# A hybrid Fourier / RWKV-7 layer on one core: a table and two token tiles get longer rows, and what else is placed moves by 128, 192 or 384 bytes

## The chip, the cores and the metric

The kernel runs on one core of a Trainium2 chip. The time is that of one execution on the device, in microseconds (us), the median of several runs: 3869.45 us for the kernel before (three runs, 3867.17 to 3881.99). A single profiled execution took 3867.45 us, and its span from the first instruction to the last is 3865.6 us.

## The reference, cut to what matters

All arithmetic is float32. One layer, 256 context tokens and 2048 latent tokens, model width 1024:

```python
hx = modulate(rmsnorm(x, norm1_g), sh1, sc1)
px = hx @ w_in                       # 1024 x 4480: recurrent columns, Fourier columns, gates
qx = rwkv_inputs(centred_shift(px[..., :RWKV_COLS], mu_prev, mu_next), lp)
hc = modulate(rmsnorm(ctx, norm1_g), csh1, csc1)
pc = hc @ w_in[:, :RWKV_COLS]        # the context needs the recurrent columns alone
yx = bidir_wkv(qx, states of the context)      # decay, kd, v, kk, a: a scan over time, both ways
fx = fourier_latent(px[..., FOURIER_START:GATE_START], rows)
f_ = sigmoid(gate_f) * (fx @ w_up_f)
r_ = sigmoid(gate_r) * (rwkv_output(yx, qx) @ w_up_r)
x = x + ga1 * ((f_ + r_) @ w_out)
hx2 = modulate(rmsnorm(x, norm2_g), sh2, sc2)
x = x + ga2 * ((silu(hx2 @ w_gate) * (hx2 @ w_up)) @ w_down)     # hidden width 2816
return rmsnorm(x, final_norm_g)
```

## The kernel before, in words

**Precision by three matmuls.** Every large product is made by `mm3` (L152 to L157). Weights and activations are each split into a high and a low part of the type float32r, and each slice k of 128 input channels takes three matmuls: high weights by high activations (L155), high weights by low activations (L156), low weights by high activations (L157). Each matmul loads its own 128 x 128 weights first. The *weights* are the stationary operand; the *moving* operand is a row of an activation tile, 512 tokens long (256 or 258 in the second token tile of the projection).

**Weights.** `load_w` (L141 to L150) brings 128 columns of a weight matrix from DRAM in pieces of four slices (`wraw`), and makes the high part on ScalarE (`whi`, L148) and the low part on VectorE (`wlo`, L149). Two buffers of each, `[128, 8, 128]`, serve the whole kernel; a slice is 512 bytes long in each partition.

**Stages, in order of time.**

- *Projection.* The 2304 tokens go in three parts of 768. In each part the normed tokens stand in two pairs of tiles: `hh`, `hl` of 512 columns (the first pair), and `hh`, `hl` of 258 columns (the second pair), eight slices k in each. They are allocated at L365. The second pair has 258 columns since the first two parts need two tokens of the next one for the shift; the matmuls take 258 columns of it for the recurrent columns (`pxps`) and 256 for the gates and Fourier columns (`fps`).
- *Scan.* The recurrence, in blocks of 128 tokens, both directions at once. Its matmuls are plain float32 with 32 to 128 columns. `pcT` (L195) is the table of the products of decays over chunks of 64 tokens: 36 chunks, two directions, four pairs of heads. The projection writes it and the scan's `state` step reads it.
- *Fourier.* Small DFT matmuls (`hps`, `p12`), then `fx @ w_up_f` (`pf`, moving tiles `fh`, `fl`) with the group norms.
- *Merge.* `c_merge` (`pr`, moving `oh`, `ol`) and `c_out` (`po`, moving `mh`, `ml`), for four blocks of 512 tokens.
- *Feed-forward.* Two blocks of 1024 tokens, each as two halves of 512. For 128 hidden columns at a time, the gate weights go over the first half and then over the second (`pgt`, 24 matmuls each), then the up weights the same way (`put`); the moving tiles are `xh`, `xl` of that half. After six or five such column groups `pd` multiplies the hidden tiles `uh`, `ul` of both halves with `w_down`.

**Where tiles stand.** Tiles are placed by pools, one after another in each partition's memory. Pools of the left side grow from the low addresses: first the constants (`pcT` and `carry` are the last of them), then the weight buffers, then the pools of single stages (Fourier, `fmp`, and `fa`, which holds `xh` and `xl` of the first half). Pools of the right side are placed against the upper end: `hp` with the normed tokens and, below it, `px` with everything else of the projection; when they are closed, `sp` of the scan, later `ep` of the merge and `ff`'s pool (second halves, `uh`, `ul`) take the same room. So a longer tile on the left moves all that follows on the left, and a longer tile in `hp` moves what lies below it in `hp` and `px`, but nothing in `sp` or `ep`.

An instruction scheduler sets the order of the projection, the Fourier stage, the merge and the feed-forward; the scan's order is written by hand.

Of the kernel before, what the change touches and what calls it, by code (L numbers as in the profile page):

```python
# [7 lines left out]
F32 = mybir.dt.float32  # L8
F32R = mybir.dt.float32r
# [7 lines left out]
TOT = SEQ + CTX  # L17
KT = 8
# [4 lines left out]
C = 64  # L23
# [17 lines left out]
def layer_kernel(ctx: ExitStack, tc, I, out_T, dbg=None):  # L41
# [3 lines left out]
    cst = ctx.enter_context(tc.tile_pool(name="cst", bufs=1))  # L45
# [38 lines left out]
    hp = hpx.enter_context(tc.tile_pool(name="hp", bufs=1, side="right"))  # L84
# [56 lines left out]
    def load_w(src, K):  # L141
        hi = wp.tile([128, KT, 128], F32R, tag="whi", name="whi", bufs=2)
        lo = wp.tile([128, KT, 128], F32R, tag="wlo", name="wlo", bufs=2)
        for k0 in range(0, K, 4):
            k1 = min(K, k0 + 4)
            raw = wp.tile([128, 4, 128], F32, tag="wraw", name="wraw", bufs=RW)[:, 0:k1 - k0, :]
            nc.sync.dma_start(raw, src[:, k0:k1, :])
            nc.scalar.activation(out=hi[:, k0:k1, :], in_=raw, func=AF.Copy)  # L148
            nc.vector.tensor_tensor(out=lo[:, k0:k1, :], in0=raw, in1=hi[:, k0:k1, :].bitcast(F32), op=ALU.subtract)  # L149
        return hi, lo  # L150
# [41 lines left out]
                fo2[64 * h2:64 * h2 + 64, :].rearrange("p (a c) -> p a c", c=128))  # L192


    pcT = cst.tile([128, TOT // C, 2, 4], F32, name="pcT")  # L195


    carry = cst.tile([128, 15, 1], F32, name="carry")
# [1 line left out]
    with ExitStack() as st:  # L200
# [148 lines left out]

        def gate_columns(ct, H, lats):  # L350
            w = load_w(I["w_in"][ct], KT)
            for (hh, hl), (l0, n) in zip(H, lats):
                if l0 is None:
                    continue
                ps = pmm.tile([128, 512], F32, tag="mm", name="fps")
                mm3(ps[:, 0:n], w, lambda k: hh[:, k, 0:n], lambda k: hl[:, k, 0:n], KT, n)
                gate_evict(fo_tile, ct, ps, l0, n)

        NP = 3
        for part in range(NP):  # L360
# [1 line left out]
            S = [px.tile([128, 768], F32R, tag=f"S{i}", name=f"S{part}_{i}", bufs=1) for i in range(4)]  # L362

            cols = [(512, 256), (258, 0)] if part == 0 else [(512, p0), (258 if part < 2 else 256, p0 + 512)]
            H = [[hp.tile([128, KT, 512 - 254 * i], F32R, tag=f"h{y}{i}", name=f"h{y}{part}_{i}")[:, :, 0:n] for y in "hl"]  # L365
                 for i, (n, _) in enumerate(cols)]
            for i, (n, b0) in enumerate(cols):
                hh, hl = H[i]
                for c0 in range(0, n - n % 256, 256):
# [7 lines left out]
            if part < 2:  # L377
                for c0 in range(p0 + 768, p0 + 1536, 256):
                    xs = load_x(c0)
                    rs = stats(xs, c0, False)  # L380
                    if c0 == p0 + 768:
                        hh, hl = [x[:, :, 256:258] for x in H[1]]
                        xe = xs[:, :, 0:2]
# [18 lines left out]
            for ci, ct in enumerate((12, 13, 0, 8, 4, 1, 9, 5, 2, 10, 6, 3, 11, 7, 14)):  # L402
# [11 lines left out]
                for i, (n, _) in enumerate(cols):  # L414
                    hh, hl = H[i]
                    ps = ppx.tile([128, 512], F32, tag="px", name="pxps", bufs=6 - NAUX)
# [45 lines left out]
                for g in ((15 + ci, 30 + ci // 3) if ci % 3 == 2 else (15 + ci,)):  # L462
                    gate_columns(g, H, lats)

# [296 lines left out]
    with ExitStack() as st:  # L761
# [5 lines left out]
        for g in range(4):  # L767
# [5 lines left out]
            for (j0, j1) in ((0, 3), (3, 7), (7, 11), (11, 15), (15, 16)):  # L773
                ps = pmm.tile([128, 512], F32, tag="mm", name="hps")
                col = 0
                for j in range(j0, j1):
                    n = 192 if j == 0 else 128
# [351 lines left out]
```

## Time and profile before

| what | before |
|---|---|
| median of three runs | 3869.45 us |
| the profiled execution, its span | 3867.45 us, 3865.6 us |
| TensorE (PE) busy | 3486.3 us, 90% |
| VectorE (DVE), ScalarE (ACT) busy | 2028.1 us (52%), 1358.3 us (35%) |
| mean granted TensorE clock | 0.932 of full speed |
| projection, 66 to 1092 us | PE busy 977.3 of 1026 us |
| scan and Fourier transforms, 1092 to 1862 us | PE busy 576.0 of 770 us |
| `pf` and group norms, 1862 to 2014 us | PE busy 122.4 of 152 us |
| merge, 2014 to 2350 us | PE busy 298.6 of 336 us |
| feed-forward, 2395 to 3842 us | PE busy 1444.0 of 1447 us |

Times of stages are from the profiled execution's start. The end of a matmul is modelled in the profile (it is pipelined, and the next one starts before it ends), so a matmul's own duration is longer than the time it takes from the stream. The time from one start to the next, here called the *step*, is read from the list of instructions in order of time.

### The profile page before, as it was taken

To read this page: it belongs to the slowest core of one execution; us is meant where nothing else is said; L and a number is where in the kernel's file an instruction comes from. 1 tells how busy PE (TensorE), PEld (TensorE's weight loads), DVE (VectorE), ACT (ScalarE), POOL (GpSimd) and SP (SyncE) were. 2 spreads that over 40 slices of the span, in tenths; PEclk is the share of its full clock that TensorE was granted. 3 is DMA by queue.
4 is the path that set the end of the run, shared out by engine and by line. 5 is a ranking of instruction groups with operands and counts; after the bars stand their busy time and mean duration, and the time that the engine had idled before them with its cause. 6 is when DMAs were issued, how large, how long until landed. Compare 5 with 4: busy or idle time off the path is not lost.

```text
span 3865.6 us, 55086 instructions
## 1 busy us (share of the span) xinstructions
PE 3486.3 (90%) x21140; PEld 2867.7 (74%) x21140; DVE 2028.1 (52%) x4005; ACT 1358.3 (35%) x2632; POOL 472.7 (12%) x865
## 2 busy tenths in 40 slices
PE   5999899999958888886789798999999999999997
PEld 5786788878847777775567676888888878888886
DVE  5577557746667777762568654223233542222325
ACT  3567456645523433332234332212111321111122
POOL 0133223213221222210110000000000000000000
PEclk9999999999977888777889899999999999999998
DMA  5454544535454455534686554111111241111112
GB/s 179 125 167 149 161 144 169 168 103 177 152 161 114 130 133 142 143 85 127 226 270 225 169 185 144 46 54 41 52 45 52 84 140 42 52 45 48 50 47 68
DMA packets 270231, 465.48 MB, mean 120 GB/s; under 512 B 84208, under 2 KB 103664, under 8 KB 269456
## 3 DMA queue, kind: packets, MB, share of 16 engines
q1 hardware_dynamic: 230336, 334.38, 27.3%
q0 software_dynamic: 39632, 127.59, 10.4%
q8 instruction: 166, 2.72, 0.3%
q14 instruction: 97, 0.79, 0.1%
HBM read 341.64 MB, written 120.21 MB: 119 GB/s over the span
## 4 chain that ended last, share of the span: by engine, by line
PE 39%; issue 7%; DMA 3%; DVE 2%; ACT 1%; POOL 0%; SPq 0%; DVEq 0%; POOLq 0%; ACTq 0%
PE pd L155 4%; PE pd L156 4%; PE pd L157 4%; PE pgt L156 4%; PE put L157 4%; PE pgt L157 4%; PE pgt L155 4%; PE put L156 4%; PE put L155 4%; DMA wraw<-w_up_f 1%; DMA gnb<-y_dr 1%; DVE wlo L149 0%; POOL x_dr L921 0%; DMA x__21736<-x_dr 0%; DVE oo L1021 0%
## 5 line engine op out<-in xcount | busy, mean ns | idle before, releaser
L148 ACT ACTIVATE whi<-wraw 128x512 fp32r<-128x512 f32 (+2 forms) x642 | 360.6, 598 | 1074.8 <-PE pd L156 353.6
L149 DVE TENSOR_TENSOR wlo<-wraw,whi 128x512 fp32r<-128x512 f32 (+2 forms) x642 | 397.7, 651 | 354.0 <-ACT whi L148 353.0
L155 PE MATMUL pgt<-xh,whi 128*128 128x512 f32 x704 | 277.7, 395 | 12.4 <-ACT xh L879 12.4
L155 PE MATMUL fps<-hh,whi 128*128 128x512 f32 (+1 forms) x800 | 284.8, 356 | 0.0
L157 PE MATMUL fps<-hh,wlo 128*128 128x512 f32 (+1 forms) x800 | 284.7, 356 | 0.0
L156 PE MATMUL fps<-hl,whi 128*128 128x512 f32 (+1 forms) x800 | 282.5, 353 | 0.0
L156 PE MATMUL pd<-ul,whi 128*128 128x512 f32 x704 | 278.0, 395 | 0.0
L157 PE MATMUL pd<-uh,wlo 128*128 128x512 f32 x704 | 277.9, 395 | 0.0
L155 PE MATMUL pd<-uh,whi 128*128 128x512 f32 x704 | 277.5, 395 | 0.0
L155 PE MATMUL put<-xh,whi 128*128 128x512 f32 x704 | 277.3, 394 | 0.0
L156 PE MATMUL put<-xl,whi 128*128 128x512 f32 x704 | 277.1, 394 | 0.0
L157 PE MATMUL put<-xh,wlo 128*128 128x512 f32 x704 | 277.1, 394 | 0.0
L156 PE MATMUL pgt<-xl,whi 128*128 128x512 f32 x704 | 276.7, 393 | 0.1
L157 PE MATMUL pgt<-xh,wlo 128*128 128x512 f32 x704 | 276.7, 393 | 0.0
L155 PE MATMUL pxps<-hh,whi 128*128 128x512 f32 (+2 forms) x720 | 250.2, 348 | 18.8 <-ACT hh L229 11.3
L156 PE MATMUL pxps<-hl,whi 128*128 128x512 f32 (+2 forms) x720 | 248.5, 346 | 7.0 <-DVE hl L230 7.0
L1007 DVE SCALAR_TENSOR_TENSOR x1f<-pd,ga2h,x1f 128x512 f32<-128x512 f32 x128 | 96.1, 751 | 293.5 <-PE pd L157 293.5
L157 PE MATMUL pxps<-hh,wlo 128*128 128x512 f32 (+2 forms) x720 | 246.4, 344 | 0.0
L997 DVE TENSOR_TENSOR tg<-tg,put 128x512 f32<-128x512 f32 x88 | 60.4, 688 | 269.0 <-PE put L157 268.9
L156 PEld LDWEIGHTS fps<-hl,whi 128*128 128x128 f32 x800 | 151.8, 190 | 25.5 <-issue 5.5
L157 PEld LDWEIGHTS fps<-hh,wlo 128*128 128x128 f32 x800 | 151.8, 190 | 24.4 <-issue 4.4
L155 PEld LDWEIGHTS fps<-hh,whi 128*128 128x128 f32 x800 | 152.1, 190 | 23.7 <-issue 4.3
(382 smaller groups left out, 7183.8 us busy)
## 6 DMA issues: line engine op xcount, KB each, us to landing
wraw<-w_in SPq DMA_DIRECT2D x210, 256.0 KB, 3.1
wraw<-w_gu SPq DMA_DIRECT2D x176, 256.0 KB, 2.8
BD<-bd_dr SPq DMA_DIRECT2D x36, 512.0 KB, 6.8
KR<-kr_dr SPq DMA_DIRECT2D x36, 512.0 KB, 7.1
wada<-w_ada SPq DMA_DIRECT2D x32, 512.0 KB, 4.8
wraw<-w_out SPq DMA_DIRECT2D x64, 256.0 KB, 3.2
wraw<-w_down SPq DMA_DIRECT2D x64, 256.0 KB, 2.7
xs<-xT POOLq DMA_DIRECT2D x15, 1024.0 KB, 6.0
```

The source lines that it names most:

```text
L148: nc.scalar.activation(out=hi[:, k0:k1, :], in_=raw, func=AF.Copy)
L149: nc.vector.tensor_tensor(out=lo[:, k0:k1, :], in0=raw, in1=hi[:, k0:k1, :].bitcast(F32), op=ALU.subtract)
L155: nc.tensor.matmul(ps, wh[:, k, :], xh(k), start=start and k == 0, stop=False)
L156: nc.tensor.matmul(ps, wh[:, k, :], xl(k), start=False, stop=False)
L157: nc.tensor.matmul(ps, wl[:, k, :], xh(k), start=False, stop=stop and k == K - 1)
L997: nc.vector.tensor_tensor(out=tg, in0=tg, in1=pu, op=ALU.mult)
L1007: nc.vector.scalar_tensor_tensor(out=x1[:, ct, :], in0=pd, scalar=ga2h[:, ct:ct + 1], in1=x1[:, ct, :], op0=ALU.mult, op1=ALU.add)
```

## The change

Two tiles get longer rows than they use. `pcT` is placed as if it had 40 chunks instead of 36: 1280 bytes in each partition instead of 1152. The second pair `hh`, `hl` of the projection gets 264 columns instead of 258: a slice is 1056 bytes long instead of 1032, a tile 8448 instead of 8256. No computed value differs, and no other line is changed. In the two built programs the order of instructions is the same, row for row, on each engine.

```diff
-    pcT = cst.tile([128, TOT // C, 2, 4], F32, name="pcT")
+    pcT = cst.tile([128, TOT // C, 2, 4], F32, name="pcT", padded_shape=[128, 40, 2, 4])
...
-            H = [[hp.tile([128, KT, 512 - 254 * i], F32R, tag=f"h{y}{i}", name=f"h{y}{part}_{i}")[:, :, 0:n] for y in "hl"]
+            H = [[hp.tile([128, KT, 512 - 248 * i], F32R, tag=f"h{y}{i}", name=f"h{y}{part}_{i}")[:, :, 0:n] for y in "hl"]
                  for i, (n, _) in enumerate(cols)]
```

What moves is the place of tiles. The built programs give each tile's byte address in a partition; here it is modulo 256. "Distance" is that of the moving row from the weights' row, modulo 256; k is the slice, 0 to 7.

| tiles | before | after | distance before | distance after |
|---|---|---|---|---|
| `whi`, `wlo` (all stages) | 96 | 224 | | |
| first pair `hh`, `hl` (projection) | 96 | 224 | 0 | 0 |
| second pair, `hh` | 96 + 8k | 224 + 32k | 8k | 32k |
| second pair, `hl` | 160 + 8k | 224 + 32k | 64 + 8k | 32k |
| `fh`, `fl` (`pf`) | 96 | 224 | 0 | 0 |
| `oh`, `ol`, `mh`, `ml` (merge) | 224 | 224 | 128 | 0 |
| `xh`, `xl` of the first half | 96 | 224 | 0 | 0 |
| `xh`, `xl` of the second half | 224 | 224 | 128 | 0 |
| `uh`, `ul` (`pd`) | 224 | 224 | 128 | 0 |
| the scan's tiles | 224 | 224 | | |

The step from one slice to the next is 2048 bytes in the 512-column tiles and 512 bytes in the weights, so their rows all lie where the tile does, modulo 256. Tiles of the projection's other work move by 384 bytes, those of the Fourier stage and the group norms by 128.

## The prediction

> **What bounds the kernel now.** I read the page first, for the share of each engine and the costliest groups; then the table of busy time by stretch; then single stretches in order of time, for the step from one matmul's start to the next; last the table of waits of TensorE.
>
> The page:
>
> ```profile
> span 3865.6 us, 55086 instructions
> PE 3486.3 (90%) x21140; PEld 2867.7 (74%) x21140; DVE 2028.1 (52%) x4005; ACT 1358.3 (35%) x2632; POOL 472.7 (12%) x865
> PEclk9999999999977888777889899999999999999998
> ```
>
> The stretches (projection; scan and Fourier transforms; `pf`; merge with `pr`; merge with `po` alone; feed-forward). After the length come busy us and instructions of each engine, the granted clock, the share of the DMA engines and GB/s:
>
> ```profile
> 66.00:1092.00 1026.00, 977.29 (x5043) 800.45 (x5043) 660.69 (x1117) 603.34 (x1091) 270.38 (x485) 0.98 0.46 150
> 1092.00:1862.00 770.00, 575.99 (x7858) 513.04 (x7858) 488.63 (x1480) 262.05 (x643) 150.17 (x274) 0.77 0.46 127
> 1862.00:2014.00 152.00, 122.42 (x492) 92.18 (x492) 97.42 (x176) 50.79 (x105) 23.18 (x40) 0.90 0.79 261
> 2014.00:2255.00 241.00, 206.38 (x857) 160.67 (x858) 173.91 (x285) 94.64 (x176) 15.47 (x26) 0.91 0.66 219
> 2255.00:2350.00 95.00, 92.19 (x387) 73.25 (x385) 46.23 (x68) 29.72 (x52) 8.65 (x16) 0.98 0.41 136
> 2395.00:3842.00 1447.00, 1443.99 (x6239) 1170.59 (x6237) 486.60 (x767) 285.77 (x523) 0.00 (x0) 1.00 0.18 56
> ```
>
> TensorE is the bound outside the scan. In the feed-forward, 37% of the span, it is busy 1444.0 of 1447 us at the full clock, with VectorE at 486.6 and ScalarE at 285.8 us, so a nanosecond taken from each matmul there is taken from the end, and no other engine is near enough to take over. In the projection it is busy 95% and in the last piece of the merge 97%. The scan and Fourier stretch (TensorE 75%, clock 0.77) is bound otherwise.
>
> A busy matmul is not a matmul at its best, though. Here is one column group of the feed-forward in order of time: the first `pgt` of the first half, the first of the second half, and the first `put`, 24 matmuls between each and the next:
>
> ```profile
> 2459.45 0.39 PE L155 MATMUL pgt<-xh,whi 128*128 128x512 f32 x1
> ...
> 2464.90 0.39 PE L155 MATMUL pgt<-xh,whi 128*128 128x512 f32 x1
> ...
> 2470.49 0.39 PE L155 MATMUL put<-xh,whi 128*128 128x512 f32 x1
> ```
>
> The same weights, the same number of columns, no wait: the first half takes 5.45 us, a step of 227.1 ns, the second 5.59 us, a step of 232.9 ns. The first half's tiles lie at 96 modulo 256 like the weights (distance 0), the second half's at 224 (distance 128). Groups of the feed-forward over its whole length say the same in the modelled durations: `pd`, whose tiles are all at distance 128, has 395 ns, and `put`, half of whose matmuls are at distance 0, 392.
>
> ```profile
> L156 PE MATMUL pd<-ul,whi 128*128 128x512 f32 x704 | 278.0, 395 | 0.0
> L157 PE MATMUL pd<-uh,wlo 128*128 128x512 f32 x704 | 277.9, 395 | 0.0
> L155 PE MATMUL pd<-uh,whi 128*128 128x512 f32 x704 | 277.5, 395 | 0.0
> L157 PE MATMUL put<-xh,wlo 128*128 128x512 f32 x688 | 269.9, 392 | 0.0
> ```
>
> **The change part by part.** No instruction, wait or transfer is added, taken away or put elsewhere in order, on any engine or queue. What can change is how long an instruction takes, by where its operands lie. The forecast rests on one reading: the step is 227 ns where the moving row and the weights are at the same offset modulo 256, and about 6 ns more at distance 128. Step by step:
>
> *`pd`.* 8 column tiles by two halves by 6 slices by 3 are 288 matmuls without a break, 287 steps in 66.97 us:
>
> ```profile
> 2503.63:2570.60 66.97, 66.97 (x288) 1.00 0.17 52
> ```
>
> That is 233.3 ns. Brought to 227.1, each of the 2112 `pd` matmuls (three lines, 704 each) gives 6.2 ns: 13.1 us, all on the path.
>
> *Second halves of `pgt` and `put`.* Half of six lines of 704, so 2112 matmuls, 5.8 ns each: 12.2 us, on the path. The first halves keep distance 0 and give nothing.
>
> *`po`.* A block is 192 matmuls, 191 steps, in 44.45 us from the first row to the last:
>
> ```profile
> 2176.76 0.39 PE L155 MATMUL po<-mh,whi 128*128 128x512 f32 x1
> ...
> 2221.21 0.40 PE L157 MATMUL po<-mh,wlo 128*128 128x512 f32 x1
> ```
>
> 232.7 ns; 5.6 ns by 768 matmuls are 4.3 us. TensorE hardly waits in this piece (97% busy), so it counts in full.
>
> *`pr`.* 384 matmuls at the same distance give 2.2 us at the most. But here TensorE waits for others between them:
>
> ```profile
> PE pr L155 <- ACT oh L160: 20.8, 4, 14.2
> PE pr L155 <- ACT whi L148: 6.5, 5, 2.6
> PE pr L157 <- DVE wlo L149: 2.7, 2, 2.3
> ```
>
> Where the next weights or the next `oh` are late, a matmul that ends earlier only waits longer. Between 0 and 2.2 us; I take 1.1, since the waits fall on few of the column tiles.
>
> *The second pair of the projection.* Its rows were at distances 8k and 64 + 8k, and come to 32k, equal for `hh` and `hl`. One group of 24 matmuls with 256 columns, and one with 258, from the first row to the one behind the last:
>
> ```profile
> 593.44 0.28 PE L155 MATMUL fps<-hh,whi 128*128 128x256 f32 x1
> ...
> 596.28 0.39 PE L155 MATMUL fps<-hh,whi 128*128 128x512 f32 x1
> ...
> 631.62 0.28 PE L155 MATMUL pxps<-hh,whi 128*128 128x258 f32 x1
> ...
> 634.52 0.39 PE L155 MATMUL fps<-hh,whi 128*128 128x512 f32 x1
> ```
>
> Steps of 118.3 and 120.8 ns, against 113.6 and 114.4 if the 227.1 ns scaled with the columns. There are 1320 and 720 of them. If every distance that is a multiple of 32 did as well as 0, this gives 4.7 ns by 1320 and 6.4 by 720: 10.8 us. If each still paid the 6.2 ns of distance 128, it would cost 1.5 ns by 1320 and give 0.2 by 720: a loss of 1.8 us. Only k = 0 reaches distance 0 for certain; the other seven slices remain apart, and the trace has no row at 32, 96 or 160. I take 2 us, nearer to the lower end, since the present distances, all different, cost about the same 5 to 6 ns as 128 does in the large tiles: the toll looks like one per matmul that is not at 0.
>
> *All else.* `pf` and the first pair stay at distance 0, the scan's tiles do not move, `pcT` is read and written as before; VectorE, ScalarE and the DMAs work on rows of the same lengths at starts that move by multiples of 64 bytes. In the feed-forward and the projection these engines have room (the stretches above), so a change of theirs by a per cent would be hidden; I take nothing.
>
> The sum: 13.1 + 12.2 + 4.3 + 1.1 + 2 = 32.7 us. The profiled execution took 3867.45 us, 2 us below the median of the runs shown; 3867.45 - 32.7 is 3834.8, and half-way to the median's scale that is 3836 us.
>
> The Trainium skill says otherwise about the cause: "TensorE: Matmul & The Clock Gate", Part 2, Step-by-step, has two independent read ports on TensorE, one for the moving operand and one for loading weights, so that loading the next weights takes no read bandwidth from the running matmul. By that rule a distance between the two can cost nothing, and only the moving row's own place is left to explain 227.1 against 232.9 ns; that is the first rival, and by it the sum would be 30 us the other way.
>
> **The rivals.**
>
> *The moving row's own place counts, not the distance.* Then rows that start at 224 modulo 256 are slow whatever the weights do, and the change brings every 512-column tile to 224: the first halves of `pgt` and `put` (2112 by 5.8 ns: 12.2 us), the first pair of the projection (2520 matmuls, 14.6 us), `pf` (384, at most 2.2, half of it hidden like `pr`), with nothing won in `pd`, `po` and the second halves. About 28 us slower: 3895. For it: in the matmuls compared here the weights always stand at 96, so own place and distance never part. Against it: the second pair's rows cover the starts from 96 to 152 (`hh`) and 160 to 216 (`hl`), nearly up to 224, and in the group of 256 columns the two are alike:
>
> ```profile
> L156 PE MATMUL fps<-hl,whi 128*128 128x256 f32 x8 | 2.2, 281 | 0.0
> L155 PE MATMUL fps<-hh,whi 128*128 128x256 f32 x8 | 2.2, 280 | 0.0
> ```
>
> A toll that came from starting shortly before a 256-byte line should grow towards 216. It does not; what those rows share is that they are not where the weights are.
>
> *Neither counts: no change.* The 6 ns could come from something that the fast tiles share by chance, the pool they stand in or the rows' distance in higher address bits. Then nothing moves and the time stays at 3868. For it: only one stage, the feed-forward, holds both kinds side by side. Against it: the first pair of the projection stands far up in the right-hand pool, at byte 180064, and `uh` at 180192, 128 bytes on; so pool and higher address bits are the same, and only the place modulo 256 differs. Here is one group of 24 on the first pair, from its first row to the one behind its last:
>
> ```profile
> 282.13 0.40 PE L155 MATMUL fps<-hh,whi 128*128 128x512 f32 x1
> ...
> 287.59 0.39 PE L155 MATMUL pxps<-hh,whi 128*128 128x512 f32 x1
> ```
>
> 5.46 us, a step of 227.5 ns, where `pd` on `uh` has 233.3; and VectorE and ScalarE are busier around it than in the feed-forward.
>
> *The lock is imperfect.* At distance 0 everywhere but in the small tiles, steps could settle between 227 and 233. Half of the sum is 16 us: 3852. This is the upper part of the first case rather than a case of its own.
>
> **How the numbers follow.** The forecast (distance counts) has 0.67, its own range being 3822 (the 10.8 us of the small tiles and all of `pr` come on top: 43 us) to 3853. No change has 0.18, own place 0.15. So 3836 is the prediction. The range from 3822 to 3872 takes in the first two cases and leaves out the third with the edges of the first. About half a per cent, 19 us, is what a measurement of this kernel can tell from no change. Faster by more than that: 0.67, less 0.02 for an imperfect lock that keeps over half of the toll, 0.65. Slower by more: 0.15, own place. Within: the rest, 0.20.
>
> **What would show it.** If the distance counts, the durations of `pd` in the groups fall from 395 to about 389, like `put` and `pgt`; the second 24 matmuls of a column group take 5.45 us instead of 5.59; a run of 288 `pd` matmuls takes 65.2 us instead of 66.97; the feed-forward's stretch is 25 us shorter, the merge's some 5, and the scan's the same to the microsecond. The forecast is wrong if the first halves come to 233 ns with everything else as before (own place), or if the steps are untouched (neither). The small tiles' part is wrong, alone, if their groups of 24 do not come out about 0.02 us shorter than 2.84 and 2.90 us. If the steps fall and the time does not, something else in the feed-forward would have to show as a wait of TensorE, where now there is 3 us in 1447.

## The result, and the profile after

| what | before | after |
|---|---|---|
| median | 3869.45 us | 3846.74 us |
| ratio, 95% interval | | 0.9935 (0.9906 to 0.9963) |
| a second set of runs: median | 3878.61 us | 3844.98 us |
| its ratio, 95% interval | | 0.9913 (0.9900 to 0.9927) |
| the profiled execution | 3867.45 us | 3840.49 us |

The changed kernel is faster, by 0.65% in the first set and 0.87% in the second, where the interval is narrower. From profile to profile it is 27.0 us. The ratios are taken over all executions of a set but the slow ones (one of the kernel before, 5028.75 us, in the first set, and one of the kernel with rows of 1280 bytes below, 5740.91 us), so they are not just the quotients of the medians.

The page of the changed kernel, the lines that answer to those of before:

```profile
span 3838.7 us, 55086 instructions
PE 3455.2 (90%) x21140; PEld 2869.3 (75%) x21140; DVE 2028.0 (53%) x4005; ACT 1357.8 (35%) x2632; POOL 477.3 (12%) x865
PEclk9999999999976878876899899999999999999998
```

VectorE, ScalarE and the instruction counts are what they were; TensorE is 31 us less busy. Its groups in the feed-forward (line, operation, shapes, count, busy us and mean ns of one, idle time before and its releaser):

```profile
L156 PE MATMUL pd<-ul,whi 128*128 128x512 f32 x704 | 274.0, 389 | 0.0
L157 PE MATMUL pd<-uh,wlo 128*128 128x512 f32 x704 | 273.9, 390 | 0.0
L155 PE MATMUL pd<-uh,whi 128*128 128x512 f32 x704 | 273.6, 390 | 0.0
L155 PE MATMUL put<-xh,whi 128*128 128x512 f32 x688 | 268.1, 390 | 0.9 <-ACT whi L148 0.9
L157 PE MATMUL put<-xh,wlo 128*128 128x512 f32 x688 | 268.0, 390 | 0.0
```

`pd` came from 395 to 389 or 390 ns, `put` from 392 to 390, and there is no difference left between them. The same column group as before, in order of time (start us, modelled duration us, what):

```profile
2458.60 0.39 PE L155 MATMUL pgt<-xh,whi 128*128 128x512 f32 x1
...
2464.04 0.39 PE L155 MATMUL pgt<-xh,whi 128*128 128x512 f32 x1
...
2469.48 0.39 PE L155 MATMUL put<-xh,whi 128*128 128x512 f32 x1
```

Both halves now take 5.44 us for 24 matmuls, a step of 226.7 ns; before it was 5.45 and 5.59. The second half's tiles did not move. They stand at 224 modulo 256 as before, and only the weights came to them.

The time of each stage, from first and last starts in the two lists of instructions (projection: first `pxps` to last `fps`; scan: from there to the last `xr`; `pf` and group norms: first `pf` to first `pr`; merge: first `pr` to last `po`; feed-forward: first `pgt` to last `pd`), with the second trace of the changed kernel beside it:

| stage, us | before | after | after, second trace |
|---|---|---|---|
| projection | 1020.7 | 1022.1 | 1019.6 |
| scan | 679.7 | 681.5 | 688.2 |
| `pf` and group norms | 151.9 | 151.8 | 148.8 |
| merge | 335.2 | 330.5 | 333.3 |
| feed-forward | 1486.8 | 1459.9 | 1460.6 |

The gain lies in the feed-forward, 26.2 to 26.9 us of it. The merge gives 4.7 and 1.9 us. The scan, in which neither an instruction nor an address of its own tiles differs, was 1.8 and 8.5 us longer; what it does from one execution to the next is taken up below.

### The profile page after: what moved, and what is told of

The parts are those of the page before. It is cut to its first block, busy times and chain, and to the rows that moved or that the text cites. A ratio compares the mean times of both kernels' runs of the same rounds, so it can differ in the third digit from the quotient of the medians.

```text
span 3838.7 us, 55086 instructions
## 1 busy us (share of the span) xinstructions
PE 3455.2 (90%) x21140; PEld 2869.3 (75%) x21140; DVE 2028.0 (53%) x4005; ACT 1357.8 (35%) x2632; POOL 477.3 (12%) x865
## 4 chain that ended last, share of the span: by engine, by line
PE 40%; DMA 5%; issue 3%; DVE 2%; ACT 1%; SPq 0%; POOL 0%; DVEq 0%; ACTq 0%; POOLq 0%
PE pd L157 4%; PE pd L156 4%; PE pd L155 4%; PE put L157 4%; PE put L155 4%; PE put L156 4%; PE pgt L156 4%; PE pgt L155 4%; PE pgt L157 4%; PE po L157 1%; PE po L156 1%; PE po L155 1%; DMA wraw<-w_up_f 1%; DMA gnb<-y_dr 1%; DMA wraw<-w_up_r 1%
```

## The experiments

The theory: the step of a 512-column matmul depends on the *distance*, the place of its moving row less that of the weights, modulo 256 bytes; 0 is quick. The rivals: the moving row's own place counts; the weights' own place counts; the change's gain is something else that moved with the tiles.

### The change again

No edit. It is the control of the next three.

> The changed kernel once more, beside the next three. Nothing new is in it. If the distance of the moving row from the weights (modulo 256 bytes) sets the step, pd has a step of 226.7 ns again and the feed-forward stretch is 27 us shorter than before. If the 5 us by which the projection, the scan and the Fourier stage came out longer in the first profile belong to the change, they show again; if they are chance, they differ.

`pd` again has 226.7 ns, the feed-forward 1460.6 us. The merge began 4.4 us later than before in the first trace of the change and 5.5 us later in this one, so the surplus shows again in its sum, but not stage by stage: the projection came out 1.1 us shorter than before (1.4 us longer in the first trace) and the scan 8.5 us longer (1.8 us in the first). In the kernel of "Another common place" below, whose distances are the same, the merge began 0.5 us earlier than before. Nothing here shows that the surplus belongs to the change.

### Each half of the change alone

```diff
 # the table alone
+    pcT = cst.tile([128, TOT // C, 2, 4], F32, name="pcT", padded_shape=[128, 40, 2, 4])
             H = [[hp.tile([128, KT, 512 - 254 * i], ...
```

```diff
 # the token tiles alone
     pcT = cst.tile([128, TOT // C, 2, 4], F32, name="pcT")
-            H = [[hp.tile([128, KT, 512 - 254 * i], ...
+            H = [[hp.tile([128, KT, 512 - 248 * i], ...
```

> The longer table alone: weights at 224, the projection's first pair stays at 96 (distance 128), while merge and feed-forward are all at distance 0. Distance counts: pd, po and all of pgt and put at 226.7 ns as with the whole change, the first pair (2520 matmuls) goes from 228.3 to about 233 ns, so the projection is some 12 us longer than before and the whole about 12 to 15 us shorter than before. Place of the weights counts (224 quick, 96 slow): the first pair stays at 227 to 228 ns, and the whole is as quick as the change, 25 us under before. Place of the moving row counts (96 quick): the first pair stays at 228 ns too.

> The longer token tiles alone: weights stay at 96, the first pair moves to 224 (distance 128), merge and feed-forward stand as before. Distance counts: first pair about 233 ns, projection 12 us longer, pd and the second halves 233 ns as before: some 12 us slower than before. Place of the weights counts: nothing differs from before. Place of the moving row counts: first pair at 233 ns as well, which run e1 tells apart.

With the table alone, 24 matmuls of the projection on the first pair, whose rows stand at 96 and the weights at 224, and a group of the feed-forward:

```profile
211.97 0.40 PE L155 MATMUL fps<-hh,whi 128*128 128x512 f32 x1
...
217.57 0.59 PE L343 MATMUL bnps<-bsq,cn 128*128 128x512 f32 x1
```

```profile
L156 PE MATMUL pd<-ul,whi 128*128 128x512 f32 x703 | 273.7, 390 | 0.0
```

With the token tiles alone, the same group of the projection, rows at 224 and weights at 96:

```profile
212.92 0.40 PE L155 MATMUL fps<-hh,whi 128*128 128x512 f32 x1
...
218.50 0.59 PE L343 MATMUL bnps<-bsq,cn 128*128 128x512 f32 x1
```

The two groups take 5.60 and 5.58 us, 233.3 and 232.5 ns a step, against 227.5 ns in the kernel before. Rows at 96 are slow with weights at 224, and rows at 224 are slow with weights at 96; in the changed kernel 224 with 224 is quick, and before it 96 with 96 was. Neither own place explains all four, and the distance does. Over all first-pair matmuls without a wait the step rose from 228.4 to 232.4 and 232.5 ns, and the projection to 1030.1 and 1030.5 us, 9 to 10 us more than before. The feed-forward is 1458.5 us with the table alone and 1486.6 with the token tiles alone: the whole gain of this stage belongs to the table, since it moves the weights to where the merge's and the feed-forward's tiles stand. The token tiles' part is to bring the projection back.

In times: the tiles alone have a ratio of 1.0019 (1.0006 to 1.0032), slower than before by some 7 us where 12 were expected; the table alone 0.9914 (0.9897 to 0.9930), which can't be told from the whole change in times. Its median is 30.9 us below that of before, where 12 to 15 were expected, in four executions that lie 26 us apart. That the table alone costs 9 us in the projection is shown by its trace and not by its runs.

### Every slice of the small tiles at distance 0

```diff
-            H = [[hp.tile([128, KT, 512 - 248 * i], ...
+            H = [[hp.tile([128, KT, 512 - 192 * i], ...
```

> The change with 320 columns instead of 264 in the second pair: rows of 1280 bytes, so all eight slices of hh and hl are at distance 0 too. If the toll is one per matmul that is not at distance 0, whatever its columns: the small tiles go from 118 to 120 ns to 113.5 and 114.4, 9.5 us off, and the first pair, disturbed by them, from 228.3 to 227 ns, 2 us more: 10 to 12 us under the change. If small tiles cost what they cost for another reason (fewer columns than a weight load takes): same as the change.

24 matmuls with 256 columns, all at distance 0:

```profile
594.22 0.28 PE L155 MATMUL fps<-hh,whi 128*128 128x256 f32 x1
...
597.09 0.40 PE L155 MATMUL fps<-hh,whi 128*128 128x512 f32 x1
```

2.87 us, a step of 119.7 ns; in the kernel before it was 118.3. After the first step, of 113 ns, it settles at 120. So distance 0 does not bring 256 columns down to half of the 512-column step, and the 10 to 12 us expected from it did not come: the ratio is 0.9922 (0.9908 to 0.9935), no better than the change. The first pair, which was to go to 227 ns as well, stayed at 228.4. The other reason that the expectation names, that a weight load takes longer than so few columns, fits two things: in this kernel 258 columns take the same 119.7 ns as 256, and the loads follow one another without idle time, which they do not with 512 columns:

```profile
L156 PEld LDWEIGHTS fps<-hl,whi 128*128 128x128 f32 x8 | 1.5, 192 | 0.0
```

```profile
L156 PEld LDWEIGHTS pgt<-xl,whi 128*128 128x128 f32 x8 | 1.5, 188 | 0.3
```

The first row is of the 24 matmuls above, the second of 24 `pgt` of the changed kernel. No run isolates it, and it leaves open why the same tiles take 118.2 ns in the changed kernel.

### The low weights moved aside

A gap of 128 bytes before and one behind `wlo`, so that `whi` and all 512-column tiles stay at 224 and `wlo` stands at 96.

```diff
     def load_w(src, K):
         hi = wp.tile([128, KT, 128], F32R, tag="whi", name="whi", bufs=2)
+        if not gaps:
+            gaps.append(wp.tile([128, 32], F32, tag="gapa", name="gapa", bufs=1))
         lo = wp.tile([128, KT, 128], F32R, tag="wlo", name="wlo", bufs=2)
+        if len(gaps) == 1:
+            gaps.append(wp.tile([128, 32], F32, tag="gapb", name="gapb", bufs=1))
```

> The change with the low weights wlo moved 128 bytes on, so they lie at 96 and whi and all moving tiles at 224. While a matmul runs, the next one's weights are loaded. If the toll comes from the matmul's distance to its own weights: only whi by xh and whi by xl are free, wlo by xh (L157) pays. If it comes from the distance to the weights that are loaded meanwhile, which are those of the next matmul: whi by xl (L156, followed by wlo) pays, L157 (followed by whi) doesn't. Either way one matmul in three: pd steps of 228 to 229 ns on average and some 15 to 23 us over the change. If only the place of the tiles as a whole matters and the pair does not: 226.7 ns.

The groups of the feed-forward (the three lines of `mm3` are L161 to L163 here):

```profile
L163 PE MATMUL pd<-uh,wlo 128*128 128x512 f32 x701 | 278.0, 397 | 0.0
L162 PE MATMUL pd<-ul,whi 128*128 128x512 f32 x701 | 277.4, 396 | 0.0
...
L161 PE MATMUL pd<-uh,whi 128*128 128x512 f32 x702 | 272.5, 389 | 0.0
```

Two of three pay. The step from `whi` by `uh` to the next is 226.7 ns; from `whi` by `ul`, in which `wlo` is loaded, 232.4; from `wlo` by `uh` 234.2. Neither of the two readings alone holds. A matmul is quick when the weights it uses and the weights loaded in its step both lie where its row does; whether the 232.4 is the loading during that step, or a late start of the matmul that follows on `wlo`, the steps don't tell. The feed-forward takes 1486.0 us, 26 us more than with the change. Time: 1.0014 (0.9995 to 1.0032), all of the gain gone, more than the 15 to 23 us expected, because two in three pay.

### A ruler

Gaps between the tiles of the feed-forward, and starts some columns inside a wider tile, put the second half of `pgt` and `put`, `pd` of the first half and `pd` of the second at three distances in one kernel. In two of them the small tiles' distance is set as well, with rows of 1280 bytes. The cut shows the gaps around `uh` and `ul` in the first of the three kernels:

```diff
-                UH = [ep.tile([128, 6, 512], F32R, tag="uh", ..., bufs=2) for hf in range(2)]
-                UL = [ep.tile([128, 6, 512], F32R, tag="ul", ..., bufs=2) for hf in range(2)]
+                UH, UL = [], []
+                for hf, gap in enumerate((16, 40)):
+                    UH.append(ep.tile([128, 6, 512], F32R, tag=f"uh{hf}", ..., bufs=1))
+                    UL.append(ep.tile([128, 6, 512], F32R, tag=f"ul{hf}", ..., bufs=1))
+                    if gap and blk2 + f0 == 0:
+                        ep.tile([128, gap], F32, tag=f"gap_{hf}", name=f"gap_{hf}", bufs=1)
```

> A ruler, made of gaps between tiles: in the feed-forward the second half of pgt and put stands at distance 64, pd of the first half at 32, pd of the second at 96, the first half of pgt and put stays at 0; the projection's second pair has rows of 1280 bytes and stands at 128 throughout. Toll for any distance but 0: 233 ns at 32, 64 and 96. Toll that grows with the distance up to 128: 228, 230, 231.5. Toll at 128 alone (both streams in the same place of a 256-byte line): 227 throughout. Small tiles: 119.7 ns if their step doesn't depend on the distance; 118 or less if 120 was the bad case at 0.

> The ruler's other half: second half of pgt and put at distance 192, pd of the first half at 160, of the second at 224; the second pair of the projection at 192. Flat toll: 233 ns throughout. Symmetric about 128: 231.5 at 160, 230 at 192, 228 at 224. Small tiles: in the changed kernel the three matmuls of a slice at distance 192 had steps of 116 to 117 ns, so 117 ns if that belongs to the distance, 119.7 if not; 117 would be 5 us for 2040 matmuls.

> The ruler once more, with small distances: second half of pgt and put at 16 bytes, pd of the first half at 8, of the second at 240 (16 short of 256). The coarse ruler had 233 at 32, 229.6 at 64, 233 to 234 from 96 to 224. Flat toll: 233 at all three. Toll that sets in only with a whole piece of 32 bytes: 227 at 8 and 16.

Each of the three was executed once (3875.19, 3885.08 and 3870.73 us), so only their steps are read. Two readings of the kind that fills the table below: 24 `put` at distance 64, from its first to the one behind the last, and the same at 192:

```profile
2443.80 0.40 PE L155 MATMUL put<-xh,whi 128*128 128x512 f32 x1
...
2449.30 0.40 PE L155 MATMUL pgt<-xh,whi 128*128 128x512 f32 x1
```

```profile
2446.09 0.39 PE L155 MATMUL put<-xh,whi 128*128 128x512 f32 x1
...
2451.69 0.39 PE L155 MATMUL pgt<-xh,whi 128*128 128x512 f32 x1
```

5.50 and 5.60 us, 229.2 and 233.3 ns. The means over all steps of a stage without a wait (those under 262 ns; 1044 to 2112 steps each, of the changed kernel for 0 and the one before for 128):

| distance, bytes | step, ns | from |
|---|---|---|
| 0 | 226.7 | `pd`, `put` |
| 8 | 233.4 | `pd` |
| 16 | 231.6 | `put` |
| 32 | 233.1 | `pd` |
| 64 | 229.6 | `put` |
| 96 | 233.2 | `pd` |
| 128 | 233.3, 233.0 | `pd`, `put` |
| 160 | 234.0 | `pd` |
| 192 | 233.3 | `put` |
| 224 | 233.2 | `pd` |
| 240 | 234.3 | `pd` |

The mean toll is 6.3 to 7.6 ns at all distances but 64 (2.9) and 16 (4.9). It neither grows up to 128 nor waits for a whole piece of 32 bytes: 8 bytes bring all of it. None of the distances tried is quicker than 0. The first halves, at distance 0 throughout, went up with their neighbours, to 227.5 to 228.8 ns in the ruler kernels: some matmuls after a change of distance still pay.

A mean is all that this table gives, for the single steps are not alike. At distance 128, in the kernel before, they alternate between about 229 and about 238 ns, in `pd` as in the second halves:

```profile
2466.29 0.40 PE L155 MATMUL pgt<-xh,whi 128*128 128x512 f32 x1
2466.53 0.39 PE L156 MATMUL pgt<-xl,whi 128*128 128x512 f32 x1
2466.76 0.40 PE L157 MATMUL pgt<-xh,wlo 128*128 128x512 f32 x1
2467.00 0.39 PE L155 MATMUL pgt<-xh,whi 128*128 128x512 f32 x1
2467.22 0.40 PE L156 MATMUL pgt<-xl,whi 128*128 128x512 f32 x1
```

To the 10 ns that the list shows, these four steps are 0.24, 0.23, 0.24 and 0.22 us. At distance 64 the second halves repeat steps of 232, 226 and 229 ns on average, at 16 of 235, 230, 228 and 234, and at 192 the three are alike, 233 to 234; all steps of `pd` in the changed kernel, at distance 0, lie between 225 and 228. So the size of the mean toll goes with a pattern over several matmuls, and the runs do not show what makes the pattern.

The small tiles, as medians over whole groups of 23 steps (21 groups with 256 columns, 9 with 258): with 256 columns 119.7 ns at distance 0, 119.7 at 128, 117.8 at 192, and 118.2 in the changed kernel, where the slices stand at eight distances; with 258 columns 119.7, 122.0, 120.9 and 119.7. A spread of 2 ns and no clear best place.

### Another common place

The table of 41 rows instead of 40, and a gap of 224 bytes at the end of each right-hand pool, so that all weights and 512-column tiles stand at 0 modulo 256.

```diff
-    pcT = cst.tile([128, TOT // C, 2, 4], F32, name="pcT", padded_shape=[128, 40, 2, 4])
+    pcT = cst.tile([128, TOT // C, 2, 4], F32, name="pcT", padded_shape=[128, 41, 2, 4])
...
+                hp.tile([128, 56], F32, tag="gapi", name="gapi")
...
+                ep.tile([128, 56], F32, tag="gapm", name="gapm", bufs=1)
...
+                    ep.tile([128, 56], F32, tag="gapf", name="gapf", bufs=1)
```

> All weights and all 512-column tiles moved together from 224 to 0 modulo 256: distances as with the change, the common place another one. If the distance alone counts: pd, po, pgt and put at 226.7 ns, a time equal to the change. If a start on a 256-byte line saves the first piece of a read, or costs one: a step under or over 226.7, each nanosecond being 10 us over the 10392 matmuls with 512 columns.

```profile
L156 PE MATMUL pd<-ul,whi 128*128 128x512 f32 x702 | 272.9, 389 | 0.0
```

226.7 ns, and 0.9920 (0.9898 to 0.9943), which can't be told from the change's own time. The common place does not count, and rows that begin on a 256-byte line win nothing over rows that begin 32 bytes ahead of one. This kernel also settles the period. In the changed kernel the rows of `pd` and their weights agree modulo 512 as well; here, by the built program's addresses, they are 256 bytes apart modulo 512, and the step is the same. 128 bytes cost 6.6 ns and 256 nothing.

### The scan from one execution to the next

The scan's instructions and its own tiles' addresses are the same in all these kernels, and its length was 679.7, 681.5, 688.2, 697.2, 684.2, 683.1, 687.6, 690.3, 694.6, 684.2 and 688.4 us in eleven traces (before, the change, then the runs in the order told, the rulers before the common place and the fine ruler last). The busy table of the whole scan, in the kernel before (the shortest), with the table alone (the longest) and in the second ruler (length, busy us and instructions of each engine, granted clock, DMA share, GB/s):

```profile
1091.40:1771.10 679.70, 528.45 (x7651) 473.80 (x7651) 470.70 (x1416) 243.89 (x598) 146.93 (x268) 0.77 0.46 124
```

```profile
1101.10:1798.20 697.10, 540.93 (x7651) 484.02 (x7651) 470.37 (x1416) 243.91 (x598) 146.90 (x268) 0.75 0.45 121
```

```profile
1091.00:1785.60 694.60, 543.11 (x7653) 488.73 (x7651) 471.14 (x1418) 243.87 (x598) 147.03 (x268) 0.74 0.44 121
```

The same 7651 matmuls keep TensorE busy for 528 us in the shortest scan and for 541 in the longest, at a granted clock of 0.77 and 0.75; VectorE and ScalarE are as busy in one as in the other. The scan at the lowest clock, 0.74, is not the longest. Whether the clock is the cause was not tried. The 17 us between shortest and longest are more than half of the change's gain, so one execution of each kernel could show well under half of the gain or over one and a half times as much. The trace of before has the shortest scan of all, so the 27.0 us from profile to profile are, if anything, a low reading. That the first set's medians give 22.7 us and the second set's 33.6 can come from this; the runs do not show that it does.

## Why the prediction was right

The forecast was 3836 us, from a sum of 32.7 us; the medians came out 22.7 and 33.6 us below theirs, the profile 27.0. The measured median of 3846.74 us lies in the range from 3822 to 3872, though the lower end is 4 us too low by its own terms: 42.6 us instead of 32.7 make 3826. The four terms of the feed-forward and the merge, 30.7 us, can be held against the stages: 31.6 us in one trace, 28.1 in the other. How near the whole came is in part luck: the scan moves by up to 17 us between executions, the small tiles gave less than their 2 us, and the first halves gave some 1.3 us that were put at nothing. Step by step:

*The first reading held:* 227 ns at equal offsets and 6 ns more at distance 128, with the distance as cause. The result itself rules out the main rival, that the moving row's own place counts: `pd` and the second halves stayed at 224 and became quick, and the first halves came to 224 and stayed quick. The two halves of the change done alone, and the common place at 0, say the same of the weights' own place. The rival that neither counts falls with the result as well, since the steps changed; and in the ruler 8 bytes are enough, in the same pools.

*`pd` and the second halves* were to give 25.3 us. The steps fell to 226.7 instead of 227.1, the first halves gained 0.6 ns too, and the feed-forward lost 26.9 and 26.2 us. The forecast had put the first halves at nothing; in the kernel before, the first three steps of each, right behind matmuls at distance 128, took 231.6 ns on average and the others 226.7. That TensorE alone bounds the stage held: of the steps' gain of 28.7 us only some 2 us turned into new waits, such as the 0.9 us of `put` for `whi` in the rows above.

*`po` and `pr`* were to give 5.4 us together. Steps of `po` fell from 232.7 to 227.0 ns as worked out; the merge as a whole was 4.7 us shorter in one trace and 1.9 in the other, its waits for `oh` and `whi` being as long as before (22.0 us for `oh` alone in the changed kernel's table of waits, 20.8 before).

```profile
PE pr L155 <- ACT oh L160: 22.0, 4, 14.4
```

*The small tiles* were the wrong step. I took 2 us of a possible 10.8, and reasoned that "the toll looks like one per matmul that is not at 0". With all slices at distance 0 they took 119.7 ns, in the median of the groups, where the kernel before had 118.4 with 256 columns and 121.1 with 258. So the 113.6 ns set as their best was reached at no distance tried, and the upper bound of 10.8 us was bare scaling. What their step of 118 to 122 ns is made of stays open. The forecast's own sign, groups 0.02 us shorter than 2.84 and 2.90 us, came for 258 columns alone, by these medians 0.03 us; with 256 the same group takes 2.84 us again. By their steps the change gave some 1.2 us, and the projection's length does not show it.

*All else at nothing* held on the mean: `pf` and the projection are within some 3 us of before, the projection in both directions. That the scan would stay "the same to the microsecond" did not hold, with 1.8 and 8.5 us more: the forecast left out how far the scan moves by itself.

With `wlo` alone moved by 128 bytes, two of three steps went from 226.7 to 232.4 and 234.2 ns: the step depends here on where the two operands lie with respect to each other. The rule of the Trainium skill that spoke against the change, "TensorE: Matmul & The Clock Gate", Part 2, Step-by-step (two independent read ports, so that loading the next weights takes no read bandwidth from the running matmul), does not hold for these matmuls if it is read as a statement on time. Whether reads are what the operands collide in, the runs do not show.

## What to carry to other kernels

Where long runs of float32r matmuls each load their own weights, put weight tiles and moving tiles at the same byte offset modulo 256; a little padding in the pool ahead of the tiles decides it, and the two tiles of a split (high and low) must both agree. It is worth 6 to 7 ns of 233 for a matmul of 512 columns at most distances and nothing certain for 256, so look first for a stage where TensorE has no waits, and compare two groups of the same stage that differ in place alone: the step from start to start shows the toll before anything is changed.

## What the runs showed of the hardware that was not expected

- The mean toll does not grow with how far apart the rows are: 8 bytes cost 6.7 ns, 128 cost 6.6, 240 cost 7.6, and 256 nothing. Only 64 bytes cost less, 2.9 ns, and 16 something between, 4.9.
- It is not paid alike by each matmul: at distance 128 steps of about 229 and 238 ns alternate, at 64 steps of 232, 226 and 229 ns repeat.
- One weight tile of two out of place slows two steps in three, the one in which it is loaded and the one in which it is used (226.7, 232.4, 234.2 ns).
- A run of 256-column matmuls at distance 0 settles at 120 ns, more than half of the 512-column step of 226.7, after a first step of 113.
- The scan's length varies by 17 us over eleven traces with the same instructions and addresses, its granted clock between 0.74 and 0.77.
